# Four DMAs in place of 32 for a quadrant swap in HBM

## The chip, the cores and the metric

One core of a Trainium2 chip. The metric is the device time of one execution, in microseconds. Most executions of a kernel agree within 0.3%; a difference counts as one from 2% on.

## The reference

```python
def setup_inputs():
    return {
        "x": np.random.randn(8192, 8192).astype(np.float32),
    }

def reference(x: np.ndarray) -> np.ndarray:
    return np.fft.ifftshift(x)
```

With even sizes this swaps the four quadrants of the matrix diagonally: 4096 x 4096 floats each, no arithmetic. A row of the matrix is 32 KB, a row of a quadrant 16 KB, in all 268 MB are read and 268 MB written.

## The kernel before

```python
STEP = 8
...
    nc = tc.nc

    R, C = x.shape
    hr = R // 2
    hc = C // 2

    dims = [[STEP * C, hr // STEP], [1, hc]]
    for c in range(STEP):
        for col in (0, hc):
            for eng, r0, h in ((nc.sync, 0, col), (nc.scalar, hr, hc - col)):
                eng.dma_start(
                    out=bass.AP(out.tensor, out.offset + (r0 + c) * C + h, dims),
                    in_=bass.AP(x.tensor, x.offset + (hr - r0 + c) * C + hc - h, dims),
                )
```

An access pattern is a list of [step in elements, count]. Each of the 32 DMAs takes every eighth row of a quadrant, 512 rows of 16 KB, straight from the input to the output in HBM. The sync engine's queue (q1 in the profile) does the upper half of the output and the scalar engine's queue (q10) the lower half, always the diagonally opposite quadrant. The launch code around this is the same in both kernels.

## Time and profile before

| | before |
|---|---|
| time, median of 3 runs | 811.68 us (811.56 to 812.05) |
| span of the profiled run, and its time | 821.3 us, 823.08 us |
| data packets of 16 KB, per DMA engine | 1024 |
| share of the 16 DMA engines, first slice to last | 9 tenths or more in all but the end |

No compute engine takes part, so of a page of this kind only the DMA rows say anything: the busy share of the 16 DMA engines (a digit is tenths, for each fortieth of the span), what they moved, and the queues. The prediction shows these rows and reads them. The profiled run took 823.08 us, 1.4% more than the timed ones (a span lies some 2 us under the time of the same run, so time is compared with time here).

A data packet is here one piece of 16 KB, half a row of the matrix, that one of the 16 DMA engines moves; a DMA has landed when all its packets are written and its semaphore, the counter that the issuing engine waits for, has been raised. How long a DMA is under way stands in the DMA view, by issuing queue, with size and median time from issue to landing:

```profile
out_dram<-in_x_dram ACTq DMA_DIRECT2D x16, 8192.0 KB, 204.3
out_dram<-in_x_dram SPq DMA_DIRECT2D x16, 8192.0 KB, 204.1
```

One lands every 51 us on each queue, so with 204 us from issue to landing about four DMAs of each queue are under way at a time.

### The profile page before, as it was taken

Reading aid. Unit: us, or ns where it says so; the run is one execution under the profiler, and the core shown is the slowest. Engines: PE = TensorE matmul, PEld = TensorE weight load, DVE = VectorE, ACT = ScalarE, POOL = GpSimd, SP = SyncE. Lnnn points to the kernel's source line nnn. Section 1 sums busy time; section 2 is a strip of 40 time slices with the busy share of each in tenths; the row PEclk is TensorE's granted clock in tenths of the full one; section 3 lists DMA queues with packets and bytes.
Section 4 is the critical chain, followed back from the end, with each engine's and each line's share of the span. In section 5 each row is a group of like instructions: output and inputs, shape, how many; then the busy total and the mean of one; then the engine's idle time right before and its main releaser. Section 6 shows DMA issues by size and latency. Waiting matters only on the chain. (4 is left out here: it accounts for less than half of the span.)

```text
span 821.3 us, 77 instructions
## 1 busy us (share of the span) xinstructions
POOL 0.2 (0%) x4
## 2 busy tenths in 40 slices
POOL 0000000000000000000000000000000000000000
DMA  9999999999999999999999999999999999999998
GB/s 304 325 328 333 326 325 330 321 329 330 325 330 330 327 328 333 329 330 330 328 328 327 334 325 330 326 326 328 331 329 330 326 332 326 328 324 333 326 328 298
DMA packets 16896, 268.44 MB, mean 327 GB/s; under 512 B 512, under 2 KB 512, under 8 KB 512
## 3 DMA queue, kind: packets, MB, share of 16 engines
q1 hardware_dynamic: 8448, 134.22, 50.2%
q10 hardware_dynamic: 8448, 134.22, 49.7%
HBM read 268.44 MB, written 268.44 MB: 654 GB/s over the span
## 5 line engine op out<-in xcount | busy, mean ns | idle before, releaser
L51 POOL MEMSET const-bfloat16-1.0<- 128x1 bf16 x1 | 0.1, 103 | 0.0
L51 POOL MEMSET const-uint8-127<- 128x1 uint8 x1 | 0.1, 102 | 0.0
L51 POOL MEMSET const-float32-0.0<- 128x1 f32 x1 | 0.1, 99 | 0.2 <-issue 0.2
L51 POOL MEMSET const-float32-1.0<- 128x1 f32 x1 | 0.1, 99 | 0.0
## 6 DMA issues: line engine op xcount, KB each, us to landing
out_dram<-in_x_dram ACTq DMA_DIRECT2D x16, 8192.0 KB, 204.3
out_dram<-in_x_dram SPq DMA_DIRECT2D x16, 8192.0 KB, 204.1
```

The source lines that it names most:

```text
L51: nc = _bacc.Bacc("TRN2", target_bir_lowering=False, num_devices=1)
```

## The change

Its intent: one plain DMA for each quadrant, two on each queue. The loop over row residues goes, and with it 28 of the 32 DMAs. Two things change with that: the number (and size) of DMAs, and the order in which rows are taken.

```diff
-STEP = 8
...
-    dims = [[STEP * C, hr // STEP], [1, hc]]
-    for c in range(STEP):
-        for col in (0, hc):
-            for eng, r0, h in ((nc.sync, 0, col), (nc.scalar, hr, hc - col)):
-                eng.dma_start(
-                    out=bass.AP(out.tensor, out.offset + (r0 + c) * C + h, dims),
-                    in_=bass.AP(x.tensor, x.offset + (hr - r0 + c) * C + hc - h, dims),
-                )
+    for eng, r0, h in (
+        (nc.sync, 0, 0),
+        (nc.scalar, hr, hc),
+        (nc.sync, 0, hc),
+        (nc.scalar, hr, 0),
+    ):
+        eng.dma_start(
+            out=out[r0 : r0 + hr, h : h + hc],
+            in_=x[hr - r0 : 2 * hr - r0, hc - h : 2 * hc - h],
+        )
```

## The prediction

> **What bounds the kernel now.** No compute engine does any of the work, so I read the DMA side first: the slices and the packet count at the head of the page, then the queues, then the bytes at the HBM.
>
> ```profile
> span 821.3 us, 77 instructions
> ...
> DMA  9999999999999999999999999999999999999998
> GB/s 304 325 328 333 326 325 330 321 329 330 325 330 330 327 328 333 329 330 330 328 328 327 334 325 330 326 326 328 331 329 330 326 332 326 328 324 333 326 328 298
> DMA packets 16896, 268.44 MB, mean 327 GB/s; under 512 B 512, under 2 KB 512, under 8 KB 512
> ## 3 DMA queue, kind: packets, MB, share of 16 engines
> q1 hardware_dynamic: 8448, 134.22, 50.2%
> q10 hardware_dynamic: 8448, 134.22, 49.7%
> HBM read 268.44 MB, written 268.44 MB: 654 GB/s over the span
> ```
>
> The reader is to see that the 16 DMA engines are busy from the first slice to the last, at one rate, and that the two queues share them evenly. The 16896 packets are 16384 data packets (268.44 MB over 16384 is 16 KB, half a row of the matrix) and 512 small ones, 16 for each of the 32 DMAs: the semaphore writes. From the shares: (50.2% + 49.7%) of 821.3 us on 16 engines is 13,128 us of engine time, over 16384 data packets 0.801 us each. An engine has 1024 of them, and 1024 x 0.801 = 820 us, which is the span. So the time is the number of 16 KB packets of an engine times the mean duration of one, and nothing else of size. The single packet records of the trace show how that mean is made: about a quarter take 0.611 us and almost none takes less, the rest spread up to 1.3 us and a few more. So 0.611 us is the pace of an engine with nothing in its way (1024 x 0.611 = 626 us) and the other 0.19 us is time in which a packet waits for memory.
>
> Then the table of stretches, to see whether the rate depends on where in the matrix the kernel is:
>
> ```profile
> core 0: us, POOL busy (x), PEclk, DMA share, GB/s
> ...
> 4.00:6.00 2.00, 0.00 (x0) 1.00 1.15 459
> ...
> 8.00:12.00 4.00, 0.00 (x0) 1.00 1.01 348
> ...
> 20.00:60.00 40.00, 0.00 (x0) 1.00 1.00 328
> ...
> 100.00:200.00 100.00, 0.00 (x0) 1.00 1.01 326
> 200.00:300.00 100.00, 0.00 (x0) 1.00 1.00 328
> ...
> 600.00:700.00 100.00, 0.00 (x0) 1.00 1.01 328
> ```
>
> A stretch of about 100 us is one round of the source's loop over c (four DMAs); the rate is the same in each within 1%, so the row residue c and the column half don't matter. Only the first microseconds are faster.
>
> Last, how the DMAs are issued: the timeline, of two short windows, and the sync queue's waits.
>
> ```profile
> 2.69 43.47 SPq L33 DMA_DIRECT2D out_dram<-in_x_dram  x1
> 3.11 48.10 ACTq L33 DMA_DIRECT2D out_dram<-in_x_dram  x1
> ```
>
> ```profile
> SPq L62 <- DMA out_dram<-in_x_dram: 167.2, 2, 118.8
> SPq L33 <- DMA out_dram<-in_x_dram: 133.8, 12, 50.6
> ```
>
> The first three DMAs of a queue are issued in some 0.6 to 0.9 us each; the fourth issue stands for 43 or 48 us. A DMA puts 512 / 16 = 32 data packets and one semaphore write on each engine, and the first DMA lands near 51 us (the semaphore's records). At the end of the fourth issue, at 46.2 us, about 29 of the first 33 are done; 4 x 33 - 29 leaves about 103 waiting per engine. I take that as the depth of the queue ahead of the engines, an estimate. So the issuing engines wait nearly all the time, for the DMA engines. They cost nothing, as the busy row shows.
>
> **What the Trainium skill says.** "DMA: Bandwidth & Descriptors", section "Issuing engines are not separate DMA queues": transfers from the scalar and sync engines run on the same 16 DMA engines and interleave, and issuing from several saves issue time only. The trace agrees: 50.2% and 49.7% of the same engines, in turns of about 16 packets, one for each engine. The same page, "Why a DMA increments its semaphore by 16 and not by 1": a DMA goes to the largest number of engines up to 16 that divides its slowest dimension, and an engine may get at most 65,535 descriptors of one. 512 rows and 4096 rows both give 16; the trace has 16 increments for each DMA. The same page, "Latency and other measured facts": copies with a row pitch of 512 KiB ran at 207 GB/s in each direction, with 4 or 8 MiB at 103. Neither pitch of this case is in that list (256 KB before, 32 KB after); the rows of this trace at 256 KB ran at 327. "HBM Reference", "Specifications (TRN2)": about 716 GB/s for an HBM domain. The page of before has 654, which is 91% of that; the one burst above it, 459 GB/s of packets between 4 and 6 us, is counted by packet starts.
>
> **The change part by part.**
> Data packets: none is removed. `out[r0:r0+hr, h:h+hc]` is 4096 rows of 4096 elements, again 16 KB pieces, 4 x 4096 = 16384 of them, 1024 for each engine.
> Semaphore writes: 4 DMAs x 16 = 64 in place of 512, 28 fewer on each engine. One takes 9 ns in the packet records, and the next data packet follows at once, of the other queue: 28 x 9 ns = 0.25 us.
> Issues: 2 on each queue for 16. The first one still takes about 0.6 us before the first packet (at 2.1 us in the trace); the later ones lay beside the transfers. Gain on the path: 0.
> Waits of an issue for an earlier DMA: 133.8 us on the sync queue go, all behind a queue about 100 packets deep, so none of it starved an engine. Gain 0. In its place the first issue will stand until all but about 103 of its 257 packets per engine are taken: 154 packets, in turns with the other queue, 154 x 2 x 0.801 = 247 us, then the second about until the first lands plus that much. Nobody needs that time.
> End: of the last DMA of each queue the 16 increments lie within 1.2 us, as close as those of the first, so engines don't drift apart when left alone. The tail stays.
> Order of addresses: this is the only part with a size. Before, one queue's next packet on an engine is 8 rows on, 256 KB; after, it is the next row, 32 KB. If an engine gets a block of consecutive rows of the DMA (no view shows it), the engines stay 8 MB apart in both: 32 x 256 KB and 256 x 32 KB. The pairs of quadrants that run together are the same too. I find nothing in before that says that the pitch costs time: the rate doesn't depend on c, and at the start, with all engines in step at the same place of their shares, the second round of packets took 0.611 us each.
> Sum: 0.25 us of 811.68, that is nothing, and the term of the address order with an expected value near zero but a wide spread.
>
> **The rivals.**
> 1. Memory likes the next row less (or more) than the eighth row on. The mean packet time is 0.19 us above the pace of a free engine, so there is something to lose or win. A packet of 0.84 us (+5%) gives 852 us; one of 0.90 us, half as much waiting again, 912 us. One of 0.76 us gives 770 us and 689 GB/s at the HBM, 96% of the skill's figure, which leaves so little room that I think a gain of this size unlikely. For a loss speaks that the kernel before looks deliberate: nobody writes a step of 8 rows with unchanged engine distance unless the plain slices had been tried. Against it, the flat rate over c and the start.
> 2. The supply of descriptors. A DMA of 257 packets per engine is more than the queue's depth of about 103, so its generation stands open for hundreds of microseconds. If one queue's open DMA keeps the other queue from being filled, the two run one after the other. The engines would then still be fed, by one queue, and the time would be 800 to 830 us. Against it: before, the two long issues lie over each other, each ending about 5 us apart, as the two queues' landings do. If descriptors were made engine by engine, the first engine would have to drain before the last gets work, and the time would be over 1200 us; against it, the 16 engines all start between 2.1 and 2.7 us. I give that 3%.
> 3. The end gets uneven. If one queue is served more, its quadrants end early, and the other goes on alone; as both feed the same engines, the sum is unchanged: 810 to 820 us.
>
> **Range and chances.** With no change of the packet time the kernel stays at 811 us. The chances of rival 1 are lopsided: I see a ceiling above and a deliberate choice below. I give 0.60 to within 2% (795 to 828 us), 0.30 to slower, mostly 830 to 900 us, and 0.10 to faster. The middle of that is about 815 us; for 8 in 10 I take 797 to 868 us.
>
> **What would show it right or wrong.** Right: 16448 packets (16384 + 64), two queues at about 50% each, the DMA row at 9 throughout, 325 to 330 GB/s in every stretch, issues of some hundreds of microseconds that no engine feels, and landings of the first two DMAs together near 410 us. Rival 1: the DMA share is still 1.00, but the GB/s of the stretches change, and the mean of a packet leaves 0.80 us; if it then depends on the stretch, the address is what matters. Rival 2: one queue's packets end before the other's begin, or a DMA row under 9 in the first quarter. Rival 3: unequal shares of the queues until one ends. The prediction is wrong if packets get longer or shorter by over 2% with the engines still full.

## The result, and the profile after

| | before | after |
|---|---|---|
| time, median of 6 runs | 811.69 us (811.4 to 812.15) | 813.33 us (811.65 to 817.56) |
| ratio, 95% interval | | 1.0025 (1.0002 to 1.0048) |
| span of the profiled run | 821.3 us | 811.0 us |
| mean of a data packet in the profiled run | 0.801 us | 0.786 us |

A ratio here and below is the mean time of one kernel's fast runs over that of the fast runs of before in the same rounds, so not quite the ratio of the medians.

The page of the changed kernel:

```profile
span 811.0 us, 47 instructions
...
DMA  9999999999999999999999999999999999999998
GB/s 305 335 333 329 331 336 331 329 334 331 332 334 335 327 335 338 333 332 332 335 335 331 330 335 335 333 338 330 325 334 332 335 331 334 335 335 330 334 335 288
DMA packets 16448, 268.44 MB, mean 331 GB/s; under 512 B 64, under 2 KB 64, under 8 KB 64
## 3 DMA queue, kind: packets, MB, share of 16 engines
q1 hardware_dynamic: 8224, 134.22, 50.3%
q10 hardware_dynamic: 8224, 134.22, 48.9%
HBM read 268.44 MB, written 268.44 MB: 662 GB/s over the span
```

The packets are 16384 + 64, as counted beforehand; the engines are as full as before, and the queues share them. Its table of stretches:

```profile
core 0: us, POOL busy (x), PEclk, DMA share, GB/s
...
4.00:6.00 2.00, 0.00 (x0) 1.00 1.12 426
...
100.00:200.00 100.00, 0.00 (x0) 1.00 1.00 331
200.00:300.00 100.00, 0.00 (x0) 1.00 1.00 334
...
600.00:700.00 100.00, 0.00 (x0) 1.00 0.99 333
```

Flat again, with a quicker start, at 331 to 334 GB/s in place of 326 to 330. Whoever compares only the two profiles reads a gain of 1.3%. The timed runs, taken in the same rounds, show none. The profile of before is of a slower execution (823.08 us by its own clock), and what made it slow is not the kernel: the experiments include that kernel once more, with a span of 809.8 us.

The second issue of each queue, in the timeline:

```profile
1.35 302.96 ACTq L30 DMA_DIRECT2D out_dram<-in_x_dram  x1
1.37 297.31 SPq L30 DMA_DIRECT2D out_dram<-in_x_dram  x1
```

The issuing engines stand for about 300 us, and the DMA engines stay as busy as before.

### The profile page after: what moved, and what is told of

It reads as the page before. It is cut to its first block, busy times and chain, and to the rows that moved or that the text cites. A ratio compares the mean times of both kernels' runs of the same rounds, so it can differ in the third digit from the quotient of the medians.

```text
span 811.0 us, 47 instructions
## 1 busy us (share of the span) xinstructions
POOL 0.2 (0%) x4
## 2 busy tenths in 40 slices
DMA packets 16448, 268.44 MB, mean 331 GB/s; under 512 B 64, under 2 KB 64, under 8 KB 64
## 3 DMA queue, kind: packets, MB, share of 16 engines
q1 hardware_dynamic: 8224, 134.22, 50.3%
q10 hardware_dynamic: 8224, 134.22, 48.9%
```

## The experiments

Theory A: the time is 1024 packets per engine times a packet time that memory sets; neither the number of DMAs nor this change of row order touches it. Rival B: both touch it, and the two effects cancel. All kernels below gave correct results. They share a helper that issues one DMA with a given pattern, written `move(engine, first output row, column, row, dims)`. The first eight ran on one chip, the last four on another; each has before beside it. The edits are shown in part: against before where they change STEP, against the run e1_next_row_32 for e12_255_apart, and else against the changed kernel, written with the helper.

### One part alone: row order of the changed kernel, 32 DMAs

```diff
+    n = 32
+    dims = [[(hr // 16) * C, 16], [C, n], [1, hc]]
+    for c in range(hr // 16 // n):
+        for col in (0, hc):
+            move(nc.sync, 0, col, c * n, dims)
+            move(nc.scalar, hr, hc - col, c * n, dims)
```

> The order of rows of the changed kernel (each engine has 256 consecutive rows of a quadrant and takes the next row each time), but cut into 32 DMAs as in the kernel before. Theory A (time = 1024 packets per engine times a packet time that memory sets, and neither the row order nor the number of DMAs touches it): 811 to 814 us, within 0.4% of before. Theory B (two effects that cancel: the row order gains about as much as the large DMAs lose): under 803 us, or over 823 us if the signs are the other way. Side question: before's profiled run took 821.3 us and its timed ones 811.7; if the many DMAs are what the profiler slows, this kernel's profiled span is also near 820 us, with about 16896 packets.

Measured: 1697.34 us, from 1621 to 1744, beside 811.47 us of before: 2.09 times by the medians. By the rule that a run over 1.5% above the kernel's fastest is slow, five of six count as slow, the profiled one among them, so there is no interval; the fastest alone is twice before. Both theories were far off. Its page:

```profile
GB/s 150 158 157 162 159 157 165 150 164 161 161 162 147 167 155 160 167 157 162 156 158 160 157 162 155 164 159 155 165 157 162 162 157 165 155 156 164 154 160 141
DMA packets 16896, 268.44 MB, mean 159 GB/s; under 512 B 512, under 2 KB 512, under 8 KB 512
...
HBM read 268.44 MB, written 268.44 MB: 317 GB/s over the span
```

The same packets as before, the engines full, and half the rate: a packet takes 1.63 us in the mean of the records. So packet time can double with nothing changed but the pattern that picks the rows. I had written this pattern with the belief of the prediction, that an engine gets a block of consecutive rows. At twice the time it can hardly be the changed kernel's order. Theory C was formed on this: a plain DMA deals its rows to the 16 engines in turn, so that neighbouring engines work 256 KB apart before and 32 KB apart after, while this pattern set them 8 MB apart.

### One queue, other neighbours: three variants of the changed kernel

```diff
-    for eng, r0, h in (...):   # sync and scalar in turn
+    for _, r0, h in (...):     # the same four, all on nc.sync
```

> The changed kernel with all four DMAs on the sync queue. Theory A: engines are fed by one queue as well as by two, so 811 to 815 us and 331 GB/s. Rival (two queues help, because one queue's packets hide something of the other's, or they hurt, because two streams of rows collide in memory; the first microseconds of both traces ran with one queue at 0.611 us a packet): over 830 us, or under 795 us.

Measured: 814.6 us, ratio 1.0051 (1.003 to 1.0073). One queue carried all of it:

```profile
q1 hardware_dynamic: 16448, 268.44, 99.1%
```

With one queue in place of two the time is half a per cent above before, inside the 2% that count. This is theory A.

```diff
-    dims = [[C, hr], [1, hc]]
+    dims = [[C, 16], [16 * C, hr // 16], [1, hc]]
```

> The changed kernel with the rows of a quadrant dealt out to the engines in turn: engines are 32 KB apart in place of 8 MB, and an engine's next packet is 512 KB on in place of 32 KB. Still four DMAs. Theory A: within 1% of 812 us. Rival (memory cares for where the 16 engines stand to each other, so 8 MB apart is worse or better than 32 KB): over 2% away from 812 us, in either direction, with the mean packet time changed by as much.

Measured: 813.6 us, ratio 1.0022 (1.001 to 1.0034). The rows dealt out explicitly behave like the changed kernel: the same 16448 packets, 331 GB/s, and even an issue that stands 297.1 us on the sync queue (297.3 in the changed kernel). That fits theory C, under which the two are the same order.

```diff
-    (nc.sync, 0, 0), (nc.scalar, hr, hc), (nc.sync, 0, hc), (nc.scalar, hr, 0)
+    (nc.sync, 0, 0), (nc.scalar, 0, hc), (nc.sync, hr, 0), (nc.scalar, hr, hc)
```

> The changed kernel with other pairs of quadrants at a time: the two queues write the left and the right half of the same rows (and read the right and left half of the same rows), in place of diagonal quadrants. Theory A: within 1% of 812 us. Rival (memory gains when both halves of a row of 32 KB are touched together, or loses because the two streams meet in the same place): over 2% away.

Measured: 812.58 us, ratio 1.0007 (0.9993 to 1.0021). Of these two ways to pair the quadrants neither is better.

### Four kernels that turned out to be others than meant

```diff
+    n = 256
+    dims = [[n * C, 16], [C, n], [1, hc]]                  # 4 DMAs
```

> The run e1_next_row_32, which I took for the row order of the changed kernel, took twice as long (1697 us). Theory C: a plain DMA of many rows deals its rows to the 16 engines in turn, so in both kernels of the study the engines are close (256 KB before, 32 KB after), while the 3-dimensional pattern of e1 put them 8 MB apart, and that distance is what memory punishes. This kernel has the four DMAs of the changed kernel with the block per engine spelled out: 16 blocks of 256 consecutive rows. Theory C: 1600 to 1800 us. Rival D (the changed kernel has blocks of 256 rows too, and e1 is slow from its many 3-dimensional DMAs): 811 to 816 us.

```diff
+    n = 255
+    dims = [[n * C, 16], [C, n], [1, hc]]                  # 4 DMAs
+    rest = [[C, hr - 16 * n], [1, hc]]                     # and 4 of 16 rows
```

> As e6_block_256, but with 255 rows per engine, so that the engines are 8 MB less 32 KB apart; a second small DMA per quadrant moves the 16 rows that are left. Each engine still walks through consecutive rows. Theory C in its narrow form (memory punishes engines that stand at the same place of an 8 MB period): 811 to 830 us. Rival E (memory punishes the walk through consecutive rows, or any far distance of the engines): 1600 to 1800 us like e6.

```diff
+    n = 32
+    dims = [[n * C, 16], [C, n], [1, hc]]                  # 32 DMAs, rows 512 * c on
```

> 32 DMAs of 512 consecutive rows each, 32 consecutive rows to an engine: the engines are 1 MB apart. Theory C says nothing firm of 1 MB: full rate (812 to 830 us) if the period that hurts is over 1 MB, 1600 us if it is 1 MB or less. My guess lies between, 900 to 1300 us, since before's 256 KB is free and 8 MB costs double. Rival E (the walk through consecutive rows): 1600 us or more.

```diff
+    dims = [[(hr // 16) * C, 16], [8 * C, 32], [1, hc]]    # 32 DMAs, rows c on
```

> The 32 DMAs of the kernel before, the same rows in each DMA, but spelled out so that an engine gets a block: rows 256e + c + 8i, engines 8 MB apart. If the kernel before already worked like that, this one takes 812 us; under theory C (its rows are dealt in turn, engines 256 KB apart) it takes 1600 to 1800 us.

Measured: 810.47, 809.81, 812.04 and 811.44 us, ratios 0.9992 (0.9978 to 1.0007), 1.0003 (0.9978 to 1.0029), 1.0008 (0.999 to 1.0027) and 1.0002 (0.9989 to 1.0015). At first sight theory C has fallen. But the listing of the built DMAs (of one queue; it is read from the built program, not from a trace) shows what was run:

```
e1  DMACopy out_dram<-in_x_dram 16x32x4096 x16
e4  DMACopy out_dram<-in_x_dram 16x256x4096 x2
e6  DMACopy out_dram<-in_x_dram 4096x4096 x2
e8  DMACopy out_dram<-in_x_dram 512x4096 x16
e9  DMACopy out_dram<-in_x_dram 512x4096 x16
```

16 blocks of n rows that lie n rows apart are one run of 16 n rows, and the builder joins them. The blocks were never there. (e7's are two of 4080 rows and two of 16.) So these say nothing of theory C, but three of them answer other questions:

- The first is the changed kernel again: on this chip 0.9992, so the +0.25% of the result does not repeat.
- The last is the kernel before again. Its profiled span is 809.8 us and its packet 0.786 us, where the first profile of that kernel had 821.3 and 0.801. So it isn't the 32 DMAs that a profile slows, the side question of the first experiment.
- The third is what I had wanted in the very first experiment: the kernel before's number of DMAs with consecutive rows, 512 of them in each. It separates the two parts of the change.

The span of that last one, then the packets and the rate of the third:

```profile
span 809.8 us, 77 instructions
```

```profile
DMA packets 16896, 268.44 MB, mean 332 GB/s; under 512 B 512, under 2 KB 512, under 8 KB 512
```

From before to the third only the order of rows changes: nothing (1.0008). From it to the changed kernel mainly the number of DMAs: nothing either (the changed kernel's repeat, in the same rounds, is 0.9992). Rival B is out: there are no two effects that cancel.

### Theory C with patterns that can't be joined

```diff
-    n = 32
-    dims = [[(hr // 16) * C, 16], [C, n], [1, hc]]
+    n, m = 255, 51
+    dims = [[n * C, 16], [C, m], [1, hc]]
-    for c in range(hr // 16 // n):
+    for c in range(n // m):
...
+    rest = [[C, hr - 16 * n], [1, hc]]    # 16 rows, once for each quadrant
```

> The last four kernels didn't test theory C: the builder joins 16 blocks of n rows, n rows apart, into one plain run of rows, so e6 was the changed kernel again, e7 nearly so, e8 the changed kernel's rows in 32 plain DMAs and e9 the kernel before. This one can't be joined: each DMA is 16 blocks of 51 consecutive rows, 255 rows apart (8 MB less 32 KB), 20 such DMAs and four of 16 rows for the rest. It differs from the slow e1_next_row_32 in 256 to 255 rows between engines and 32 to 51 rows of a block. Theory C, narrow (engines at the same place of a period of 8 MB): 808 to 830 us. Rival E (the 3-dimensional form with consecutive rows per engine, or any far distance): over 1500 us. If C holds, plain DMAs of rows can't give their engines blocks 8 MB apart, so they deal rows in turn.

Measured: 854.61 us, ratio 1.0405 (1.0379 to 1.043). Its page:

```profile
DMA packets 16768, 268.44 MB, mean 315 GB/s; under 512 B 384, under 2 KB 384, under 8 KB 384
...
HBM read 268.44 MB, written 268.44 MB: 629 GB/s over the span
```

One row less between the blocks, 8 MB - 32 KB in place of 8 MB, takes the time from twice before to 4% above it. So neither the 3-dimensional form, nor the far distance, nor a walk through consecutive rows costs that much by itself; what is left is the round distance. Two more things differ between the pair: blocks of 51 rows for 32, and 24 DMAs for 32 (and the chip, worth 1.3% in before). The number of DMAs is free by the runs above; that the longer blocks don't count was not tested alone. The expectation of at most 830 us was missed: 4% is left, and no run tells whether the blocks of 51 rows, the distance or the 24 DMAs hold it.

```diff
-STEP = 8
+STEP = 32
```

> The kernel before with a step of 32 rows: 128 plain DMAs of 128 rows, 1 MB apart. Rows dealt in turn put the engines 1 MB apart, and theory C expects something between before (256 KB, 812 us) and e1: my guess is 850 to 1300 us. If plain DMAs gave blocks, the engines would stay 8 MB apart whatever the step, and this kernel would take 812 us as before does.

Measured: 1075.2 us, ratio 1.3084 (1.3054 to 1.3113), inside the guess. The last sentence of the expectation goes too far: if plain DMAs gave blocks, the step would still set how far apart an engine's own rows are (256 KB before, 1 MB here), so this run alone doesn't rule blocks out.

```diff
-STEP = 8
+STEP = 128
```

> The kernel before with its step of 8 rows raised to 128: 512 plain DMAs of 32 rows that are 4 MB apart. If plain DMAs deal their rows in turn, the engines are 4 MB apart here, and theory C expects about the time of e1, 1400 to 1750 us (if the period is 4 MB or less; 812 to 850 us if only 8 MB hurts, and then the pairs of engines 8 MB apart would hurt a little). Rival (the distance in a plain DMA doesn't matter): the time of e11_dealt_512, which has the same number and size of DMAs.

Measured: 2915.73 us, ratio 3.5022 (3.4824 to 3.522, from the two of four runs that count as fast); its profiled run, with a span of 2950.3 us, counts as slow (3.0% above the fastest). The control with the same number and size of DMAs, but consecutive rows:

```diff
-    dims = [[C, hr], [1, hc]]             # 4 DMAs
+    dims = [[C, 32], [1, hc]]             # 512 DMAs, rows 32 * c on
```

> The row order of the changed kernel in 512 plain DMAs of 32 consecutive rows, two packets for each engine. Theory A (the number of DMAs costs nothing while the engines' queues are never empty): 256 issues of about 0.62 us on each queue are 159 us, far less than 812; four DMAs outstanding on a queue are 8 packets per engine, two queues 16, at 0.8 us each 12.8 us of work[...]. So 811 to 820 us. Rival (small DMAs leave the engines short of work, or 8192 semaphore writes show): over 828 us. It is also the control for e2_step_128.

Measured: 822.15 us, ratio 0.9994 (0.9977 to 1.0011). Before itself took 822.24 us on this chip, 1.3% more than on the other, which is why the time lies above the 811 to 820 us expected and the ratio does not. The three pages, the step of 32 first, then 128, then the control:

```profile
DMA packets 18432, 268.44 MB, mean 249 GB/s; under 512 B 2048, under 2 KB 2048, under 8 KB 2048
```

```profile
DMA  4786768777697999999999999999866887779778
GB/s 90 96 91 90 94 91 93 94 96 92 92 92 91 92 91 88 92 88 91 92 85 91 88 92 82 89 92 85 91 86 91 95 91 93 92 96 94 89 96 86
DMA packets 24580, 268.50 MB, mean 91 GB/s; under 512 B 8192, under 2 KB 8192, under 8 KB 8192
```

```profile
DMA packets 24580, 268.50 MB, mean 327 GB/s; under 512 B 8192, under 2 KB 8192, under 8 KB 8192
```

In the control, 8192 semaphore writes and 256 issues on each queue cost nothing: theory A holds down to two packets per engine and DMA. Its sync engine waits for 673 us of the 821, in steps short enough to keep the queues filled, as the view of the sync queue's waits shows:

```profile
SPq L25 <- DMA out_dram<-in_x_dram: 673.0, 252, 3.7
```

With a step of 128 the same DMAs take 3.5 times as long, more than I had expected. The packets take 2.43 us in the mean of its records, and the engines are not always full: 4 to 9 tenths in the first third, 6 to 8 for most of the last. It is tempting to add these two up, but the table of stretches forbids it:

```profile
core 0: us, POOL busy (x), PEclk, DMA share, GB/s
10.00:100.00 90.00, 0.00 (x0) 1.00 0.50 92
1000.00:2000.00 1000.00, 0.00 (x0) 1.00 0.99 89
```

With the engines half busy and with all of them busy, the same 90 GB/s pass. The packets make up the difference: 1.41 us each in the first stretch, 2.90 us in the second, by the packet records. More busy engines bring no more bytes here, so a DMA share of 1.00 does not say that the engines are the limit, and the idle engines are no second loss beside the long packets. What holds the rate at 90 GB/s, and why the engines are full at some times and not at others, stays open.

In sum, with the distance between rows that neighbouring engines hold at the same time. For plain DMAs that is the distance if rows are dealt in turn; no record names the engine of a packet:

| kernel | rows apart | ratio to before |
|---|---|---|
| changed kernel, and 512 DMAs of its rows | 32 KB | 1.0025 and 0.9994 |
| before (step 8) | 256 KB | 1 |
| step 32 | 1 MB | 1.31 |
| step 128 | 4 MB | 3.50 (two fast runs) |
| 16 blocks, 256 rows apart | 8 MB | 2.09 (medians) |
| 16 blocks, 255 rows apart | 8 MB - 32 KB | 1.04 |

With the steps of 32 and 128 two distances grow: the one between engines, and the one from an engine's row to its own next, 16 times as much if rows are dealt. Only the pair of the last two rows changes the first and leaves the second at 32 KB, and there the first decides. Every kernel reads and writes by the same pattern, so no run tells which of the two sides minds.

Theory C explains the plain kernels through dealing. If a plain DMA gave blocks, the changed kernel's engines would stand 8 MB apart like those of the fifth row, and it would take twice as long. That it doesn't, and that dealing written out explicitly takes the same time, is the evidence; it is strong, but it is inference. Dealing in small groups of rows, which no run tells from single rows, would fit too and would multiply the distances of the plain kernels in the table.

No kernel beat both: 809.81 us (1.0003) is the lowest median of all, and inside the noise.

## Why the prediction was right

**What bounds the kernel.** Right: 1024 packets times a mean packet time. All kernels at full rate have that, with 0.78 to 0.79 us a packet on the first chip of the experiments. That the order of addresses can lengthen a packet is now shown: the mean went to 1.63 us (8 MB) and 2.43 us (4 MB). That the 0.19 us above 0.611 us in the good orders is a wait for memory, as the prediction says, is not shown. And with the step of 128 the sum reads backwards: 1024 x 2.43 is 2493 us of 2950, and the packets are as long as the rate of 90 GB/s makes them. Also, 0.801 us came from a profile of a slower execution, and 820 us was its span, not the timed 811.7. For that reason the packets of the two profiles differ by 1.9%, just under the 2% that the prediction named as its sign of being wrong, though the kernels are equal. The second chip of the experiments, where before takes 822 us, suggests that the profile came from such a chip; which one it was is not recorded.

**Semaphore writes, issues, waits: 0.25 us.** Right, and by a wide margin: 512 and 8192 semaphore writes in place of 64 gave the same time.

**What stands in the place of the waits.** Wrong in form, without effect. The prediction had the first issue stand for 247 us. The first returned after 0.58 us and the second stood for 297 us. The depth of 103 packets that it used is not a constant: with 257 packets in a DMA, about 190 per engine are done on that queue when the second issue returns (packet records), which leaves 2 x 257 - 190 = 324. With all DMAs on one queue 187 are done at that point, so 327 are left. What sets it stays open.

**Landings near 410 us, even shares, even end.** The semaphore's records have them at 404.7 and 409.6 us; queues at 50.3% and 48.9%. The 16 increments of the last DMAs lie within 2.3 us, against 1.2 us before. The run with 32 DMAs of consecutive rows has 2.3 us too, so the wider end goes with the row order and not with the size of the DMAs; the microsecond is lost in the noise. The stretches ran at 331 to 334 GB/s, not at 325 to 330, which were those of the slower execution.

**Order of addresses: near zero with a wide spread.** The number was right: from every eighth row to consecutive rows, with the 32 DMAs kept, the ratio is 1.0008. One part of its reason was wrong. "If an engine gets a block of consecutive rows of the DMA (no view shows it), the engines stay 8 MB apart in both" is the step, marked as unseen but relied on: in the run written to put engines 8 MB apart the time doubled. What the runs support is that they stand 256 KB apart before and 32 KB after, if rows are dealt singly, so the distance did change, and both distances happen to run at the full rate. That is luck: the prediction didn't see that the distance changes, and a change to 1 MB costs 31%. The flat rate over the row residue, which the prediction used against rival 1, only said that shifting all engines together costs nothing; it could not say what their distance costs.

**The rivals.** Rival 1 was the right place for the risk: the same knob at 32 is 31% slower. "nobody writes a step of 8 rows with unchanged engine distance unless the plain slices had been tried" spoke for the 0.30 on slower, and the runs give no reason for the step at all. A slip without weight: its 689 GB/s for a packet of 0.76 us is scaled from the slower profile; at the 770 us it names, 537 MB make 697 GB/s. Rivals 2 and 3 did not occur: the engines are full from the first slice, the two queues' first DMAs land within 5 us of each other, and one queue alone does as well (1.0051).

## What to carry to other kernels

When the DMA engines are full and each DMA leaves them a queue of work, the count of DMAs, semaphores and queues was free in these kernels, down to two packets of 16 KB per engine; don't expect time from merging them. But full engines may only be waiting: compare the rate, not the busy share. What is not free is which addresses the 16 engines touch at the same moment: try the distance between neighbouring rows of a DMA in small steps; here 1, 4 and 8 MB cost 31% to 250%, and 8 MB less 32 KB cost 4%. And look at the built shape of a pattern before you believe an experiment on it, and at the timed runs before you believe a per cent between two profiles.

## What the Trainium skill lacked or had wrong

- "DMA: Bandwidth & Descriptors", "Why a DMA increments its semaphore by 16 and not by 1", says how many engines a DMA uses, not which rows each gets; the page has a formula for that for a transfer to 128 partitions, and none for rows in HBM. For plain HBM to HBM DMAs of many rows the runs fit rows dealt in turn: 813 us where a pattern of blocks 8 MB apart takes 1697 us.
- The same page, "Latency and other measured facts", gives rates by the row pitch of the tensors. In all kernels here that pitch is 32 KB; what counted was which rows the access pattern moves at the same time: 249 GB/s at 1 MB, 91 at 4 MB, 159 at 8 MB, 315 at 8 MB - 32 KB (distances as in the table above). Its remark that padding the pitch by a few KB restores the full rate was not tried here; what was tried, 32 KB less than 8 MB, came to within 4% of before.
- That row is also the only place I found with rates of HBM to HBM copies, and it calls 214 GB/s in each direction full. The kernels in a good order have 330 to 333 GB/s in each direction on one core, some 662 GB/s together in the changed kernel, 92% of the 716 GB/s that "HBM Reference", "Specifications (TRN2)", states for a domain.
- No page that I read says how many packets a queue takes before an issue stands: about 103 per engine with 33 in a DMA, about 324 with 257.
- No page that I read says that chips differ: the same kernel took 811.5 us on one and 822.2 us on another. What made the difference is not known.
